# Order of the mixers turned: MLA and NSA after S5, both GDN halves last, with a new arena map

## The chip, the cores and the metric

One core of a Trainium2 chip runs the whole program. The metric is device time in microseconds (us) of one execution; lower is better. Engines by their names in the profile: PE (TensorE matmul), PEld (its weight loads), DVE (VectorE), ACT (ScalarE), POOL (GpSimd), SP (SyncE, which issues the DMAs).

## The reference, cut to what matters

Two layers, each with a token mixer and a gated convolutional MLP ("FFN") between sandwich norms. 256 tokens, width 2048, all f32. In the token mixer one projection feeds four independent groups, and one output projection takes all four:

```python
proj = h @ w_in
(cq, ckv, kpe, u_s5, nq, kc, vc, ks, vs, kw, vw, ngate, gq, gk, gv, gz, ga, gb) = split_cols(proj, IN_SIZES)
o_a = mla_mixer(cq, ckv, kpe, ...)      # latent attention: two norms, q and kv up-projections, softmax attention
o_b = s5_mixer(u_s5, ...)               # diagonal complex scan
o_c = nsa_mixer(nq, kc, vc, ks, ...)    # compressed, selected and window attention, gated
o_d = gdn_mixer(gq, gk, gv, gz, ga, gb) # conv+silu of q, k, v; chunked gated delta rule; out norm * silu(gz)
o = concat([rms_norm(o_a), rms_norm(o_b), rms_norm(o_c), o_d]) @ w_out
```

The four groups depend on `proj` alone, so any order of them computes the same.

## The kernel before, in words

**Big products.** Weights come in blocks of 512 KB (`wload`, SP's queue, 4 buffers `raw`), are split into a high and a low part (`split`: ACT casts, L423; DVE subtracts, L424; 3 buffers each) and go through PE three times (`mm3`). A *unit* here is a pair of 128-column blocks of `w_in` (`gemm_b`, L709): 16 k-steps x 2 x 3 = 96 matmuls of 256 columns into one of the four PSUM banks `mm`. A 512-column token-major product (`gemm_a`, L743) is two units. Per layer: U 2 units, GDN's q, k, v 6, its gate GZ 2, CQ 2.5, NQ 2, the shared kv columns 3.3. The output projection (`project_out`, L1548) is 32 blocks of 12 matmuls of 512 columns, in two halves `jp`; in each half the four groups come in a fixed order, and all four banks are held until the last group is done.

**Mixers** (`mixers`, L1473). S5 first, then the kv products, GDN's decay gates and NSA's compression of keys and values (`nsa_compress`, L914), then `gdn_half` (L1078) for heads 0, 1 and for heads 2, 3, then `mla` (L830), `nsa` (L962), and the GZ products with `gdn_out_gate` (L1218). In layer 0 the first two U units and three of GDN's units (`FIRST`) are computed in the opening, interleaved with the conditioning products, and their convolutions (`conv_silu`, L1025) come before S5; in layer 1 one of GDN's units is.

**What sets the order.** The program's order gives each instruction its priority; the scheduler that lays down each engine's fixed queue takes what is ready, earliest in the program first. Weight loads and splits are raised above the rest. Small PSUM work draws from `self.mx()` (L233): lane 0 and lane 1 have two banks each, and with `self.lane = None` the calls alternate, beginning with lane 1. GDN half 0 and MLA are on lane 0, GDN half 1 on lane 1; NSA starts on lane 1 and turns to None (L1005) before its window attention. From there it draws ten banks: six in `attn_probs`, two for its output, and `ss` and `R` of its norm (`norm_T`, L762). Small SBUF tiles come from pools of two buffers per name and width; the three row norms of a GDN half (`normed(1)`, `normed(0)`, the output norm; `row_rs`, L557) all take `rv`, `ry`, `ra` of width 4, those of MLA, NSA and S5 the same of width 2.

**Arena.** One SBUF tensor is mapped by hand. GDN half 0 and S5 share `A_GA`, half 1 and NSA share `A_GB`; MLA lies over `A_SIL0` and `A_GA`, so it waits for half 0, as NSA waits for half 1. Conditioning of later blocks (`ada`, DVE multiply-adds with a DMA each) is fed in by `tick` (L406), at rates per weight load, per GDN product and per attention step.

```python
        for hp in range(2):
            self.lane = hp
            self.gdn_half(l, hp, self.reg((A_GA, A_GB)[hp], 6160), qkv(hp), G, on[hp])
```

Of the kernel before, what the change touches and what calls it, by code (L numbers as in the profile page):

```python
# [12 lines left out]
F32 = mybir.dt.float32  # L13
# [3 lines left out]
AF = mybir.ActivationFunctionType  # L17
ALU = mybir.AluOpType
# [14 lines left out]
O_CQ, O_CKV, O_KPE, O_U, O_NQ, O_KC = 0, 384, 640, 704, 1216, 1728  # L33
O_NG, O_GQ, O_GK, O_GV, O_GZ, O_GA = 2496, 2508, 3020, 3532, 4044, 4556
# [16 lines left out]
A_SIL0 = A_KVT + 1704  # L51
A_GA = A_SIL0 + 1536
# [7 lines left out]
A_GP = A_SIL1  # L60
FIRST = (O_U, O_U + 256, O_GQ, O_GK, O_GV)
PAIRS = FIRST + tuple(c + 256 for c in FIRST[2:]) + (O_GZ, O_GZ + 256, O_CQ, O_CQ + 256)
TOKEN_MAJOR = (((O_KC, 426),), ((O_KC + 426, 354), (O_GA, 8), (O_KPE, 64)), ((O_NQ, 512),))
# [41 lines left out]
def blocks():  # L105

    B = {nm: Blocks() for nm in ("w_in", "w_out", "ffn_w_in", "ffn_w_out", "w_ada", "mla_w_uq", "mla_w_ukv")}
    for c0 in PAIRS:
        for k0 in range(0, KT, 4):
            B["w_in"].add(k0, 4, (c0, 256))  # L110
    for k0 in range(0, KT, 8):
        B["w_in"].add(k0, 8, (O_CQ + 512, P))
    for segs in TOKEN_MAJOR:
# [79 lines left out]
class Ker:  # L193
# [515 lines left out]
    def gemm_b(self, l, c0, nm=2):  # L709


        return self.finish(self.gemms_b(l, [(c0, self.mmt())], nm, KT))[0]

# [7 lines left out]

    def gemms_b(self, l, cols, nm, kc, tiles=False):


        kn = 1024 // (nm * P)
        parts = [[b[:, m * 256:(m + 1) * 256] for m in range(nm)] for _, b in cols]
        for kk in range(0, KT, kc):
            for (c0, _), ps in zip(cols, parts):
                for k0 in range(kk, kk + kc, kn):
                    w = self.wtile(self.blk("w_in", l, k0, kn, (c0, nm * P)))  # L730
                    for ki in range(kn):
# [182 lines left out]
    def nsa_compress(self, l, r, kvt, kT, kc, vb):  # L914


        nc, I = self.nc, self.I
        scr = r(192)
        for tt in range(2):
            v = kvt[:, tt, 0:768].rearrange("p (a b) -> p a b", a=3)[:, :, 0:32]  # L920
            self.rope(scr, v, v, self.rcos[:, tt, 32:48], self.rsin[:, tt, 32:48], 3, 16)
        kcT, vT = r(256), r(256)
        for j, o in ((KV_KC, kcT), (KV_VC, vT), (KV_KS, kT[:, 0]), (KV_KW, kT[:, 1])):
# [4 lines left out]
        for nm, src in (("k", kcT), ("v", vT)):  # L928
            w2 = r(P)
            nc.sync.dma_start(w2, I["nsa_w2_" + nm][l])  # L930
            st = r(16, 18)
# [7 lines left out]
            ab = r(256)[:18]  # L939
# [4 lines left out]
            a = r(2, 18)  # L944
# [3 lines left out]
            h, g = r(16), r(16)  # L948
            nc.vector.memset(h, 0.0)
# [268 lines left out]
    def gdn_out_gate(self, ps, out):  # L1218

        nc = self.nc  # L1220
        th = self.small.tile([P, 256], F32, name="gth", tag="gth")
        nc.scalar.activation(th, ps, AF.Tanh, scale=0.5)
        nc.vector.scalar_tensor_tensor(th, th, 1.0, ps, op0=ALU.add, op1=ALU.mult)
        nc.vector.tensor_tensor(out, out, th, op=ALU.mult)

# [241 lines left out]
    def first_gemms(self, l):  # L1467
        if l:
            return self.gemms_b(l, [(c, self.mmt()) for c in FIRST[:3]], 2, KT // 4)
        self.lane = 0  # L1470
        return self.gemms_b(l, [(c, self.mmt() if i < 4 else self.mx()) for i, c in enumerate(FIRST)], 2, KT // 4, True)

    def mixers(self, l, first):  # L1473
# [5 lines left out]
        Uc = r5(8, P)  # L1479
        u0, u1, *first_qkv = self.finish(first)  # L1480
        us = (u0, u1)
        for c2, ps in enumerate(us):
            for j in range(2):
                self.s5_gather(Uc, ps[j], 2 * c2 + j)

        def conv(hp, i, ps):
            s = self.reg((A_SIL0, A_SIL1)[hp] + i * 512, 512)(2, 256)
            for j in range(2):
                self.conv_silu(l, ps[j], 4 * i + 2 * hp + j, s[:, j])
            return s  # L1490

        early = [conv(0, i, ps) for i, ps in enumerate(first_qkv)] if l == 0 else []
        self.lane = 0
# [13 lines left out]
        self.lane = 1  # L1507
        self.nsa_compress(l, self.reg(A_OT + 1024, 3072), kvt, kT, kc, vb)

        def qkv(hp):  # L1510
            sil = list(early) if hp == 0 else []
            for i in range(len(sil), 3):
                sil.append(conv(hp, i, first_qkv[i] if i < len(first_qkv) and hp == 0 else
                                self.gemm_b(l, (O_GQ, O_GK, O_GV)[i] + hp * 256)))
            return sil


        on = [oT["gdn"][:, hp * 512:(hp + 1) * 512] for hp in range(2)]
        for hp in range(2):
            self.lane = hp  # L1520
            self.gdn_half(l, hp, self.reg((A_GA, A_GB)[hp], 6160), qkv(hp), G, on[hp])

        self.lane = 0
        cqn = [oT["mla"][:, j * 256:(j + 1) * 256] for j in range(4)]
        cqn.append(self.ar[:, A_GB + 6160:A_GB + 6416])
        for c, nm in ((0, 2), (2, 2), (4, 1)):
            ps = self.gemm_b(l, O_CQ + c * P, nm=nm)
            for j in range(nm):
                nc.scalar.copy(cqn[c + j], ps[j])
        self.mla(l, cqn, self.reg(A_SIL0, 7696), kvt, oT["mla"])  # L1530
# [239 lines left out]
```

## Time and profile before

| | us |
|---|---|
| median of 3 runs | 2710.53 (2709.11 to 2710.61) |
| the profiled execution: its time / span of its instructions | 2708.32 / 2706.5 |
| PE busy / PEld busy | 2579.7 (95%) / 2283.8 (84%) |
| DVE busy / ACT busy | 1909.8 (71%) / 1258.6 (47%) |
| mean granted TensorE clock | 0.979 of full |

The span runs: opening to about 200 us, mixers and output projection of layer 0 to 640, its FFN to about 1420, mixers and output projection of layer 1 to 1920, its FFN to the end. Busy time of PE is time covered by at least one matmul, so it is not PE at its peak. A mean over the span mixes these stages; the mixers are read stretch by stretch below.

### The profile page before, as it was taken

Reading aid. Unit: us, or ns where it says so; the run is one execution under the profiler, and the core shown is the slowest. Engines: PE = TensorE matmul, PEld = TensorE weight load, DVE = VectorE, ACT = ScalarE, POOL = GpSimd, SP = SyncE. Lnnn points to the kernel's source line nnn. Section 1 sums busy time; section 2 is a strip of 40 time slices with the busy share of each in tenths; the row PEclk is TensorE's granted clock in tenths of the full one; section 3 lists DMA queues with packets and bytes.
Section 4 is the critical chain, followed back from the end, with each engine's and each line's share of the span. In section 5 each row is a group of like instructions: output and inputs, shape, how many; then the busy total and the mean of one; then the engine's idle time right before and its main releaser. Section 6 shows DMA issues by size and latency. Waiting matters only on the chain. (4 is left out here: it accounts for less than half of the span.)

```text
span 2706.5 us, 44498 instructions
## 1 busy us (share of the span) xinstructions
PE 2579.7 (95%) x17604; PEld 2283.8 (84%) x17604; DVE 1909.8 (71%) x3018; ACT 1258.6 (47%) x2001; POOL 10.2 (0%) x22
## 2 busy tenths in 40 slices
PE   7889998888999999999998999999899999999998
PEld 3468787767999999988787879888799999998886
DVE  7348877778887777776877888865777655555555
ACT  2334354555545444444545445465544444444443
POOL 0000000000000000000000000000000000000000
PEclk9989999889999999999999999999999999999999
DMA  8676666676887888876676567735587655555554
GB/s 316 245 261 217 223 211 208 205 267 219 294 299 275 282 292 295 286 252 232 232 262 219 186 206 256 247 126 179 178 279 275 212 186 180 186 180 187 187 188 147
DMA packets 171264, 620.89 MB, mean 229 GB/s; under 512 B 19440, under 2 KB 20272, under 8 KB 169520
## 3 DMA queue, kind: packets, MB, share of 16 engines
q1 hardware_dynamic: 170048, 617.00, 66.2%
q8 instruction: 138, 2.26, 0.3%
q10 hardware_dynamic: 1008, 1.06, 0.1%
q14 instruction: 70, 0.57, 0.1%
HBM read 613.75 MB, written 4.23 MB: 228 GB/s over the span
## 5 line engine op out<-in xcount | busy, mean ns | idle before, releaser
L228 PE MATMUL mm<-ht,wh 128*128 128x256 f32 x7168 | 1316.5, 284 | 6.2 <-ACT ht L423 6.2
L423 ACT CAST wh<-raw 128x1024 fp32r<-128x1024 f32 (+1 forms) x740 | 771.7, 1044 | 964.1 <-PE mm L228 794.6
L424 DVE TENSOR_TENSOR wl<-raw,wh 128x1024 fp32r<-128x1024 f32 (+1 forms) x740 | 896.1, 1214 | 409.9 <-ACT wh L423 407.4
L228 PEld LDWEIGHTS mm<-ht,wh 128*128 128x128 f32 x7168 | 1112.8, 189 | 23.0 <-ACT ht L423 9.0
L228 PE MATMUL mm<-ht,wl 128*128 128x256 f32 x3584 | 1018.1, 284 | 0.1
L228 PEld LDWEIGHTS mm<-ht,wl 128*128 128x128 f32 x3584 | 677.5, 189 | 10.9 <-issue 6.3
L228 PE MATMUL mm<-wh,ht 128*128 128x512 f32 (+1 forms) x1600 | 504.2, 394 | 7.2 <-ACT ht L423 4.5
L462 DVE SCALAR_TENSOR_TENSOR acc<-rawa,condc,acc 128x1024 f32<-128x1024 f32 x300 | 384.5, 1282 | 148.1 <-DMA rawa<-in_w_ada_dram 146.7
L228 PEld LDWEIGHTS mm<-wh,ht 128*128 128x128 f32 x1600 | 300.7, 189 | 71.5 <-ACT ht L423 4.8
L228 PE MATMUL mm<-wl,ht 128*128 128x512 f32 (+1 forms) x800 | 314.9, 394 | 1.0 <-DVE wl L424 1.0
L228 PE MATMUL mx<-wh,ht 128*128 128x512 f32 x704 | 222.3, 396 | 0.0
L228 PE MATMUL mx<-arena 128*128 128x128 f32 (+8 forms) x1432 | 200.8, 284 | 9.9 <-ACT arena L1464 2.9
L228 PEld LDWEIGHTS mx<-arena 128*128 128x128 f32 (+5 forms) x1432 | 158.7, 173 | 51.0 <-issue 15.4
L228 PEld LDWEIGHTS mm<-wl,ht 128*128 128x128 f32 x800 | 151.4, 189 | 33.5 <-DVE wl L424 2.2
L228 PEld LDWEIGHTS mx<-wh,ht 128*128 128x128 f32 x704 | 132.6, 188 | 32.3
L228 PE MATMUL mx<-wl,ht 128*128 128x512 f32 x352 | 139.7, 397 | 0.8 <-DVE wl L424 0.8
L424 DVE TENSOR_TENSOR ht<-arena,ht 128x1024 fp32r<-128x1024 f32 x52 | 63.6, 1223 | 39.9 <-ACT ht L423 39.6
L1607 DVE SCALAR_TENSOR_TENSOR arena<-mm,vec,arena 128x255 f32<-128x255 f32 (+1 forms) x176 | 78.3, 476 | 6.2 <-ACT arena L1605 5.3
L228 PEld LDWEIGHTS mx<-wl,ht 128*128 128x128 f32 x352 | 66.3, 188 | 17.3 <-DVE wl L424 1.2
L423 ACT CAST ht<-arena 128x1024 fp32r<-128x1024 f32 x52 | 54.1, 1049 | 56.7 <-PE mm L228 31.4
L228 PE MATMUL mx<-rawm,arena 128*18 128x256 f32 (+3 forms) x248 | 74.5, 494 | 2.1 <-DMA rawm<-in_w_ada_dram 1.3
L232 PE MATMUL mx<-ident,arena 128*128 128x128 f32 (+1 forms) x328 | 59.7, 286 | 11.5 <-ACT arena L807 5.6
(315 smaller groups left out, 1550.6 us busy)
## 6 DMA issues: line engine op xcount, KB each, us to landing
raw<-in_ffn_w_in_dram SPq DMA_DIRECT2D x352, 512.0 KB, 4.3
rawa<-in_w_ada_dram SPq DMA_DIRECT2D x344, 512.0 KB, 5.0
raw<-in_ffn_w_out_dram SPq DMA_DIRECT2D x176, 512.0 KB, 4.3
raw<-in_w_in_dram SPq DMA_DIRECT2D x116, 512.0 KB, 4.3
raw<-in_w_out_dram SPq DMA_DIRECT2D x64, 512.0 KB, 4.2
raw<-in_w_in_dram SPq DMA_DIRECT2D x32, 426.0 KB, 4.1
rawm<-in_w_ada_dram SPq DMA_DIRECT2D x20, 512.0 KB, 6.0
acc<-in_w_ada_dram SPq DMA_DIRECT2D x20, 512.0 KB, 6.9
```

The lines of the kernel that those rows point to most:

```text
L228: self.nc.tensor.matmul(out, lhsT=lhsT, rhs=rhs, start=start, stop=stop)
L232: self.nc.tensor.transpose(out, in_, self.ident[:k, :k])
L423: self.nc.scalar.copy(hi.bitcast(F32R), src)
L424: self.nc.vector.tensor_sub(lo.bitcast(F32R), src, hi)
L462: self.nc.vector.scalar_tensor_tensor(acc, w, self.condc[:, kc:kc + 1], acc, op0=ALU.mult, op1=ALU.add)
L1607: nc.vector.scalar_tensor_tensor(c[:, s:], ps[m][:, :256 - s], self.fconv(l, 2 - s, f), c[:, s:], op0=ALU.mult, op1=ALU.add)
```

## The change

After it the order is: U and CQ in the opening (layer 0 all of CQ, layer 1 its first unit), S5, kv products, compression, the rest of CQ, NQ, `mla` (lane 0), `nsa` (lane 1), then the six GDN units with their convolutions, both `gdn_half` (lane 0, lane 1), GZ, and one multiply per half by the gate. MLA and NSA get regions of their own (`A_MLA`, `A_NSA`), and the GDN halves take those regions over. Compression works in `A_SIL0` with one set of scratch for keys and values, and its small matrix comes through `rawm` in place of a direct load. The 128-column block of CQ is loaded in four pieces in place of two. The output projection takes NSA before GDN. `mla`, `nsa` and `gdn_half` themselves are not touched.

```diff
-FIRST = (O_U, O_U + 256, O_GQ, O_GK, O_GV)
+FIRST = ((O_U, 2), (O_U + 256, 2), (O_CQ, 2), (O_CQ + 256, 2), (O_CQ + 512, 1))
+A_MLA, A_NSA, A_SILB = A_GA, A_GA + 6656, A_GA + 12544
+A_GATE = (A_GA + 5888, A_SILB + 1536)
...
-    for k0 in range(0, KT, 8):
-        B["w_in"].add(k0, 8, (O_CQ + 512, P))
+    for k0 in range(0, KT, 4):
+        B["w_in"].add(k0, 4, (O_CQ + 512, P))
...
     def nsa_compress(self, l, r, kvt, kT, kc, vb):
-        scr = r(192)
+        STN = 18
+        kcT, vT, st_, ab_, rest = r(256), r(256), r(16 * STN), r(256), r(72)
+        scr = st_
...
-            w2 = r(P)
-            nc.sync.dma_start(w2, I["nsa_w2_" + nm][l])
...
+            w2 = self.mload(I["nsa_w2_" + nm][l])
...
     def gdn_out_gate(self, ps, out):
         nc = self.nc
-        th = self.small.tile([P, 256], F32, name="gth", tag="gth")
-        nc.scalar.activation(th, ps, AF.Tanh, scale=0.5)
-        nc.vector.scalar_tensor_tensor(th, th, 1.0, ps, op0=ALU.add, op1=ALU.mult)
-        nc.vector.tensor_tensor(out, out, th, op=ALU.mult)
+        nc.scalar.activation(out, ps, AF.Tanh, scale=0.5)
+        nc.vector.scalar_tensor_tensor(out, out, 1.0, ps, op0=ALU.add, op1=ALU.mult)
...
     def first_gemms(self, l):
         if l:
-            return self.gemms_b(l, [(c, self.mmt()) for c in FIRST[:3]], 2, KT // 4)
+            return self.gemms_b(l, [c + (self.mmt(),) for c in FIRST[:3]], KT // 4)
...
     def mixers(self, l, first):
-        u0, u1, *first_qkv = self.finish(first)
+        cqn = [oT["mla"][:, j * 256:(j + 1) * 256] for j in range(4)] + [oT["gdn"][:, 0:256]]
+        u0, u1, *done = self.finish(first)
...
-        early = [conv(0, i, ps) for i, ps in enumerate(first_qkv)] if l == 0 else []
+        for i, ps in enumerate(done):
+            latents(i, ps)
         self.lane = 0
         self.s5(l, r5, Uc, oT["s5"])
...
-        self.nsa_compress(l, self.reg(A_OT + 1024, 3072), kvt, kT, kc, vb)
-        for hp in range(2):
-            self.lane = hp
-            self.gdn_half(l, hp, self.reg((A_GA, A_GB)[hp], 6160), qkv(hp), G, on[hp])
-        self.lane = 0
-        for c, nm in ((0, 2), (2, 2), (4, 1)):
-            ps = self.gemm_b(l, O_CQ + c * P, nm=nm)
-            for j in range(nm):
-                nc.scalar.copy(cqn[c + j], ps[j])
-        self.mla(l, cqn, self.reg(A_SIL0, 7696), kvt, oT["mla"])
-        self.lane = 1
+        self.nsa_compress(l, self.reg(A_SIL0, 1536), kvt, kT, kc, vb)
+        for i in range(len(done), 3):
+            latents(i, self.gemm_b(l, *FIRST[2 + i]))
         nq = oT["nsa"].rearrange("p (a b) -> p a b", a=2)
         ps = self.gemm_a(l, TOKEN_MAJOR[2])
         for tt in range(2):
             nc.scalar.copy(nq[:, tt], ps[tt])
-        self.nsa(l, self.reg(A_GB, 6160), nq, kvt, kT, kc, vb, oT["nsa"])
+        self.lane = 0
+        self.mla(l, cqn, self.reg(A_MLA, 6656), kvt, oT["mla"])
+        self.lane = 1
+        self.nsa(l, self.reg(A_NSA, 5888), nq, kvt, kT, kc, vb, oT["nsa"])
+
+        sil = []
+        for hp in range(2):
+            r = self.reg((A_SIL0, A_SILB)[hp], 1536)
+            sil.append([])
+            for i, c0 in enumerate((O_GQ, O_GK, O_GV)):
+                ps = self.gemm_b(l, c0 + hp * 256)
+                t = r(2, 256)
+                for j in range(2):
+                    self.conv_silu(l, ps[j], 4 * i + 2 * hp + j, t[:, j])
+                sil[hp].append(t)
+        on = [oT["gdn"][:, hp * 512:(hp + 1) * 512] for hp in range(2)]
+        for hp in range(2):
+            self.lane = hp
+            self.gdn_half(l, hp, self.reg((A_MLA, A_NSA)[hp], 5888), sil[hp], G, on[hp])
         self.lane = None
+        gate = []
         for hp in range(2):
+            gate.append(self.reg(A_GATE[hp], 512)(512))
             ps = self.gemm_b(l, O_GZ + hp * 256)
             for j in range(2):
-                h = 2 * hp + j
-                og = oT["gdn"][:, h * 256:(h + 1) * 256]
-                self.gdn_out_gate(ps[j], og)
+                self.gdn_out_gate(ps[j], gate[hp][:, j * 256:(j + 1) * 256])
+        for hp in range(2):
+            nc.vector.tensor_tensor(on[hp], on[hp], gate[hp], op=ALU.mult)
...
     def project_out(self, l, oT):
-        order = (("s5", 4), ("mla", 0), ("gdn", 12), ("nsa", 8))
+        order = (("s5", 4), ("mla", 0), ("nsa", 8), ("gdn", 12))
```

## Rows read from the trace of the kernel before

**Rows 1.** Windows, layers 0 and 1: us, then busy PE, PEld, DVE, ACT, POOL, clock, DMA.

```profile
425.00:505.00 80.00, 70.35 (x468) 58.22 (x467) 60.27 (x157) 37.16 (x94) 0.96 (x1) 0.94 0.59 202
...
505.00:586.00 81.00, 62.53 (x379) 51.51 (x378) 63.42 (x160) 45.13 (x108) 2.27 (x2) 0.85 0.72 246
...
1605.00:1716.00 111.00, 110.03 (x892) 100.86 (x891) 93.52 (x168) 63.13 (x133) 0.53 (x1) 1.00 0.78 262
...
1716.00:1786.00 70.00, 69.06 (x498) 59.23 (x498) 54.76 (x144) 32.32 (x72) 0.00 (x0) 1.00 0.63 212
...
1786.00:1853.00 67.00, 66.83 (x458) 58.13 (x458) 37.66 (x103) 45.64 (x112) 0.00 (x0) 1.00 0.37 129
```

**Rows 2.** Timeline, layer 0, norms of the GDN halves: start us, us, engine, line.

```profile
359.54 0.27 ACT L652 ACTIVATE junk<-mx 128x128 bf16<-128x128 f32 x1
...
410.46 0.16 DVE L559 TENSOR_SCALAR rv<-mx 128x4 f32<-128x4 f32 x1 [2.45 <-PE mx L228]
...
410.54 0.16 DVE L559 TENSOR_SCALAR rv<-gss 128x4 f32<-128x4 f32 x1
```

**Rows 3.** Timeline, layer 1, DVE: the same two norms.

```profile
1702.84 0.16 DVE L559 TENSOR_SCALAR rv<-mx 128x4 f32<-128x4 f32 x1
...
1702.91 0.16 DVE L559 TENSOR_SCALAR rv<-gss 128x4 f32<-128x4 f32 x1
```

**Rows 4.** Timeline, layer 0, PE and ACT at the front of NSA.

```profile
504.68 1.06 PE L228 MATMUL mx<-nkc,arena 128*128 128x16 f32 x8 [0.19 <-DVE arena L1216]
...
505.54 0.57 ACT L978 COPY arena<-mx 128x512 f32<-128x512 f32 x1
...
519.91 0.31 PE L232 MATMUL mx<-ident,arena 128*128 128x128 f32 x1
...
520.06 0.96 PE L228 MATMUL mx<-nkc,arena 128*128 128x16 f32 x8
...
525.25 0.64 PE L228 MATMUL mx<-arena 128*128 128x128 f32 x2
```

**Rows 5.** Timeline, layer 0, DVE: where row norms begin (rv) and end (ry).

```profile
330.58 0.16 DVE L256 SCALAR_TENSOR_TENSOR ry<-ra,ry 128x2 f32<-128x2 f32 x1
...
423.50 0.15 DVE L256 SCALAR_TENSOR_TENSOR ry<-ra,ry 128x4 f32<-128x4 f32 x1
...
427.40 0.16 DVE L559 TENSOR_SCALAR rv<-mx 128x2 f32<-128x2 f32 x1 [1.61 <-PE mx L228]
...
500.88 0.15 DVE L256 SCALAR_TENSOR_TENSOR ry<-ra,ry 128x4 f32<-128x4 f32 x1
...
525.27 0.16 DVE L256 SCALAR_TENSOR_TENSOR ry<-ra,ry 128x2 f32<-128x2 f32 x1
...
581.62 0.16 DVE L256 SCALAR_TENSOR_TENSOR ry<-ra,ry 128x2 f32<-128x2 f32 x1
```

**Rows 6.** Timeline, layer 1, DVE: the same row norms.

```profile
1602.68 0.16 DVE L256 SCALAR_TENSOR_TENSOR ry<-ra,ry 128x2 f32<-128x2 f32 x1
...
1713.18 0.16 DVE L256 SCALAR_TENSOR_TENSOR ry<-ra,ry 128x4 f32<-128x4 f32 x1
...
1719.30 0.16 DVE L559 TENSOR_SCALAR rv<-mx 128x2 f32<-128x2 f32 x1 [1.57 <-PE mx L228]
...
1784.29 0.16 DVE L256 SCALAR_TENSOR_TENSOR ry<-ra,ry 128x4 f32<-128x4 f32 x1
...
1817.95 0.16 DVE L256 SCALAR_TENSOR_TENSOR ry<-ra,ry 128x2 f32<-128x2 f32 x1
...
1852.50 0.16 DVE L256 SCALAR_TENSOR_TENSOR ry<-ra,ry 128x2 f32<-128x2 f32 x1
```

**Rows 7.** Chain that ended last, layer 1, output projection: start us, us, what.

```profile
1853.49 35.37 PE mm L228 x151
```

**Rows 8.** Line 1032, convolutions of GDN: duration ns min/median/max.

```profile
L1032 DVE SCALAR_TENSOR_TENSOR arena<-mx,vec,arena x6: 471/476/478, 198.8 to 211.4; 128x255 f32<-128x255 f32 x2, 128x254 f32<-128x254 f32 x2, 128x253 f32<-128x253 f32 x2
```

**Rows 9.** DMA issues: KB each, median us to landing.

```profile
arena<-in_nsa_w_k_dram SPq DMA_DIRECT2D x2, 64.0 KB, 3.9
```

More of the change, by code (lines that the diff above doesn't have):

```diff
@@ L60 @@
 A_GP = A_SIL1
-FIRST = (O_U, O_U + 256, O_GQ, O_GK, O_GV)
-PAIRS = FIRST + tuple(c + 256 for c in FIRST[2:]) + (O_GZ, O_GZ + 256, O_CQ, O_CQ + 256)
+FIRST = ((O_U, 2), (O_U + 256, 2), (O_CQ, 2), (O_CQ + 256, 2), (O_CQ + 512, 1))
+PAIRS = (O_U, O_U + 256, O_CQ, O_CQ + 256) + tuple(c + d for c in (O_GQ, O_GK, O_GV, O_GZ) for d in (0, 256))
+A_MLA, A_NSA, A_SILB = A_GA, A_GA + 6656, A_GA + 12544
+A_GATE = (A_GA + 5888, A_SILB + 1536)
 TOKEN_MAJOR = (((O_KC, 426),), ((O_KC + 426, 354), (O_GA, 8), (O_KPE, 64)), ((O_NQ, 512),))
@@ L709, in gemm_b @@
     def gemm_b(self, l, c0, nm=2):
-        return self.finish(self.gemms_b(l, [(c0, self.mmt())], nm, KT))[0]
+        return self.finish(self.gemms_b(l, [(c0, nm, self.mmt())], KT))[0]
     @staticmethod
@@ L720, in finish, with gemms_b @@
                 return e.value
-    def gemms_b(self, l, cols, nm, kc, tiles=False):
-        kn = 1024 // (nm * P)
-        parts = [[b[:, m * 256:(m + 1) * 256] for m in range(nm)] for _, b in cols]
+    def gemms_b(self, l, cols, kc, tiles=False):
+        parts = [[b[:, m * 256:(m + 1) * 256] for m in range(nm)] for _, nm, b in cols]
         for kk in range(0, KT, kc):
[L728 to L731, printed above, removed]
+            for (c0, nm, _), ps in zip(cols, parts):
+                for k0 in range(kk, kk + kc, 4):
+                    w = self.wtile(self.blk("w_in", l, k0, 4, (c0, nm * P)))
+                    for ki in range(4):
                         k = k0 + ki
@@ L928, in nsa_compress @@
         for nm, src in (("k", kcT), ("v", vT)):
-            w2 = r(P)
-            nc.sync.dma_start(w2, I["nsa_w2_" + nm][l])
-            st = r(16, 18)
+            st = st_.rearrange("p (q n) -> p q n", n=STN)
             nc.vector.tensor_copy(st[:, :, 0:16], src.rearrange("p (m q) -> p q m", q=16))
@@ L938, in nsa_compress @@
                     self.mm(acc[:18], st[:, q0 + q], raw[:, q * 256:(q + 1) * 256], q0 + q == 0, q0 + q == 15)
-            ab = r(256)[:18]
+            w2 = self.mload(I["nsa_w2_" + nm][l])
+            ab = ab_[:18]
             nc.scalar.copy(ab, acc[:18])
@@ L943, in nsa_compress @@
                 self.tp(psT[:, i * 32:i * 32 + 18], ab[:, i * P:(i + 1) * P])
-            a = r(2, 18)
+            a = rest[:, 0:36].rearrange("p (i n) -> p i n", i=2)
             nc.vector.tensor_copy(a, psT[:, 0:64].rearrange("p (i n) -> p i n", i=2)[:, :, 0:18])
@@ L947, in nsa_compress @@
             nc.vector.tensor_tensor(pc, a[:, 0, 16:17], a[:, 1, 17:18], op=ALU.add)
-            h, g = r(16), r(16)
+            h, g = rest[:, 36:52], rest[:, 52:68]
             nc.vector.memset(h, 0.0)
@@ L1468, in first_gemms @@
         if l:
-            return self.gemms_b(l, [(c, self.mmt()) for c in FIRST[:3]], 2, KT // 4)
+            return self.gemms_b(l, [c + (self.mmt(),) for c in FIRST[:3]], KT // 4)
         self.lane = 0
-        return self.gemms_b(l, [(c, self.mmt() if i < 4 else self.mx()) for i, c in enumerate(FIRST)], 2, KT // 4, True)
+        return self.gemms_b(l, [c + (self.mmt() if i < 4 else self.mx(),) for i, c in enumerate(FIRST)], KT // 4, True)
     def mixers(self, l, first):
@@ L1479, in mixers, with latents @@
         Uc = r5(8, P)
-        u0, u1, *first_qkv = self.finish(first)
-        us = (u0, u1)
-        for c2, ps in enumerate(us):
+        cqn = [oT["mla"][:, j * 256:(j + 1) * 256] for j in range(4)] + [oT["gdn"][:, 0:256]]
+        u0, u1, *done = self.finish(first)
+        for c2, ps in enumerate((u0, u1)):
             for j in range(2):
                 self.s5_gather(Uc, ps[j], 2 * c2 + j)
[L1486 to L1490, printed above, removed]
-        early = [conv(0, i, ps) for i, ps in enumerate(first_qkv)] if l == 0 else []
+        def latents(i, ps):
+            for j, p in enumerate(ps):
+                nc.scalar.copy(cqn[2 * i + j], p)
+        for i, ps in enumerate(done):
+            latents(i, ps)
         self.lane = 0
@@ L1507, in mixers @@
         self.lane = 1
-        self.nsa_compress(l, self.reg(A_OT + 1024, 3072), kvt, kT, kc, vb)
[L1510 to L1518, printed above, removed]
-        for hp in range(2):
-            self.lane = hp
-            self.gdn_half(l, hp, self.reg((A_GA, A_GB)[hp], 6160), qkv(hp), G, on[hp])
-        self.lane = 0
-        cqn = [oT["mla"][:, j * 256:(j + 1) * 256] for j in range(4)]
-        cqn.append(self.ar[:, A_GB + 6160:A_GB + 6416])
-        for c, nm in ((0, 2), (2, 2), (4, 1)):
-            ps = self.gemm_b(l, O_CQ + c * P, nm=nm)
-            for j in range(nm):
-                nc.scalar.copy(cqn[c + j], ps[j])
-        self.mla(l, cqn, self.reg(A_SIL0, 7696), kvt, oT["mla"])
-        self.lane = 1
+        self.nsa_compress(l, self.reg(A_SIL0, 1536), kvt, kT, kc, vb)
+        for i in range(len(done), 3):
+            latents(i, self.gemm_b(l, *FIRST[2 + i]))
         nq = oT["nsa"].rearrange("p (a b) -> p a b", a=2)
```

1 line of the change is left out of this document (removed).

## The prediction, made before the changed kernel was run

> **What bounds the kernel now.** The windows of PE over the mixers come first, because the change moves work only there. In layer 1 PE is busy 110.0 of 111, 69.1 of 70 and 66.8 of 67 us [rows 1]: product work fills nearly every wait, and an order of the mixers can give back some 2 us. In layer 0 it is busy 70.4 of 80 and 62.5 of 81 us, 28.1 us idle, at a clock of 0.94 and 0.85: here a chain of dependent small steps decides.
>
> Next I read that chain by its row norms, each of which ends a mixer. Layer 0 [rows 5]: S5 330.58, GDN half 0 423.50, half 1 500.88, MLA 525.27, NSA 581.62. Layer 1 [rows 6]: 1602.68, 1713.18, 1784.29, 1817.95, 1852.50. So from S5 to NSA the stages are 92.9 + 77.4 + 80.7 = 251.0 us and 110.5 + 71.1 + 68.2 = 249.8 us. The two halves stand one behind the other, though they have different banks, regions and inputs.
>
> The third view, the timeline around that seam, says why. In layer 0 the squares of half 1's first norm are done at 359.8, but the norm's first step on DVE starts at 410.54, 0.08 us after the first step of half 0's *output* norm at 410.46 [rows 2]. In layer 1 the same pair is 0.07 us apart, at 1702.84 and 1702.91 [rows 3]. Both draw `rv` of width 4 from a pool of two. Half 0's first `rv` was long free; half 1's (the fourth of that name) is still not handed out before the third. I read this as: buffers of one name are handed out strictly in program order. The PSUM lanes show it too. At the front of NSA the second token tile's scores (520.06) start right behind the transpose of the first tile (519.91), though their query was copied at 505.54 and one bank of the lane was free; the first selected attention follows at 525.25 [rows 4].
>
> **The change part by part.**
>
> *The halves at the end.* `gdn_half` and its names are unchanged, so half 1 still starts its first norm at half 0's output norm. "Side by side" remains one after the other. Half 1 costs 77.4 or 71.1 us from norm to norm; I take 72, the stretch with less in its way, for it will run last, against few competitors.
>
> *Half 0 behind NSA.* Half 0 draws from lane 0. NSA, before it in the program, turns to alternating lanes for its second attention: six banks, two for its output, `ss` and `R`; beginning with lane 1, the tenth, `R`, is on lane 0 in layer 0. By the rule just read, half 0's first transposes wait for `R`, so for NSA's last norm, though its region is free when MLA ends. In layer 1 the count may put `R` on lane 1, and half 0 starts at `ss`, somewhat sooner; I put nothing for that. From its start half 0 takes between 71.1 (half 1 in layer 1) and 110.5 (half 0 there, under the full load of products); I take 78, nearer the light end, since GDN's units are done by then and GZ and the output projection are left.
>
> *MLA beside NSA.* MLA took 97.9 and 98.7 us from the start of its first norm to the end of its last [rows 5, 6], with half 1 ahead of it in priority. Now it is first: above 99, below 79 (a fifth off, about the spread of half 0 between the layers, 92.9 to 110.5, taken as what load does to such a chain). I take 85. NSA's scores and selected attention run beside it on lane 1, but the window attention needs lane 0 behind MLA's last bank. From MLA's last norm to NSA's took 34.6 us in layer 1 and 56.4 in layer 0, where the selected attention came late; I take 35.
>
> *Sum of the chain.* 85 + 35 + 78 + 72 = 270 us from S5's norm to half 1's, against 251.0 and 249.8: **+19** and **+20** us. All lower ends give 79 + 35 + 71 + 71 = 256 (+5, +6), all upper ends 99 + 56 + 110 + 77 = 342 (+91, +92).
>
> *What hides in it.* A matmul of 512 columns takes 35.37/151 = 0.234 us in the output projection [rows 7], so one of 256 some 0.117, a unit 11.2 and a group of a projection half (48 matmuls) 11.2. Six GDN units (67 us) can run early, four of them in the free banks during S5. What can run under the halves is GZ (22 us) and three groups of the projection's first half (34 us). In layer 1 that no longer fills two stretches of 70 to 80 us: PE should idle there for tens of us, where it idled 2.
>
> *The convolutions.* In layer 0 six of them leave the place ahead of S5: 6 x 4 operations of 0.476 us [rows 8] = 11.4 us of DVE. S5's chain lives on DVE, so it can end up to 11 us sooner; lower bound nothing, I take 8. The opening also loses half a unit (5.6 us of PE) to a later stage; the opening has idle PE, the later stage is held by its chain, so it is put at nothing, and at 5.6 if PE binds there.
>
> *Small edits.* Two more, smaller loads of CQ per layer move the same bytes. The small compression matrix goes through `rawm` behind four large loads instead of directly: it holds one of two buffers for a while, and the second set of weights then comes through one buffer; a load lands in 3.9 us [rows 9], so some 4 x 3.9 = 16 us later at worst, all under S5's chain; without that cover NSA's front would be 16 us late. Shared scratch for keys and values puts the second behind the first under the same cover. On SP's queue the reload of `x` and the gate row now wait for the halves instead of MLA and NSA; weight loads are raised ahead of them, as before. The gate product shrinks to one multiply per half beside the same split that followed NSA's norm: nothing.
>
> *Sum.* +19 - 8 + 20 = +31 us on the profiled execution's 2708.3, 2739 us; it stood 2.2 us below the median, so I predict 2741.
>
> A rule speaks about how much PE has to give. The PEld column covers 109.7 of the 161 us of layer 0 and 218.2 of the 248 us of layer 1 [rows 1], less than PE does. The Trainium skill, Perfetto Trace Analysis, "Identifying the Most-Contended Engine", says that matmul busy time is no measure of the distance to the limit and weight-load busy time is; no run here yet shows which of the two is right for these stretches.
>
> **The rivals.**
>
> 1. *The halves do overlap* (another order of allocation would do). For it: regions, banks and inputs are separate. Against it: the pairs 0.08 and 0.07 us apart [rows 2, 3]. The pair would cost one loaded half: 85 + 35 + 110 = 230, so -21 - 8 in layer 0 and at most -2 in layer 1: 2680 on the median. Chance 0.08.
> 2. *Fill decides, not the chain*: GDN's units fill MLA's and NSA's waits, and layer 0's 28.1 idle us are recovered; 2682. It ends on the faster side. It decides if PE stays busy under the last half, which needs products left over for it. For it: layer 1 is filled today. Against it: the work is spent earlier. Chance 0.10.
> 3. *The ends cancel*: the low end of the chain, 256 us: +5 - 8 + 6 = +3, 2714, which is no change. Chance 0.14.
> 4. *Hidden slack*: PE waits inside its busy time, and denser filling under MLA and NSA recovers it. At most 51.3 + 29.8 = 81 us [rows 1], 2629; against it, a block of 512-column matmuls runs back to back at 0.234 us [rows 7]. It is the case that the skill's rule above would make. Chance 0.04.
>
> **How the numbers follow.** Forecast, slower: 0.64, own range 2716 to 2790 (the upper ends of both layers are not reached together; I take somewhat under half of +183). A measurement of this kernel can tell about 0.2%, 5.4 us, from no change. Faster 0.08 + 0.10 + 0.04 = 0.22, same 0.14, slower 0.64. The range 2681 to 2790 takes in rivals 2 and 3; rivals 1 and 4 and some 0.06 above it are left out.
>
> **What would show it.** Right: half 1's first `rv` again starts within 0.1 us of half 0's output norm in both layers; half 0's first norm begins only after NSA's last in layer 0; PE busy falls well under 90% during half 1 in layer 1, at a lower clock; the MLA stretch is under 97.9 us. Wrong: norms of the two halves that interleave (rival 1), or PE above 95% in the last stretch (rival 2). If S5 in layer 0 ends no sooner than before against the opening, the 8 us fall; if MLA's stretch is longer than 99 us, the priority argument does.

## The result: 79 us slower, a ratio of 1.028

The kernel after took 2789.5 us (median of four runs, 2784.0 to 2792.7), beside 2710.6 for the kernel before on the same chip: a ratio of 1.0282, 95% interval 1.0259 to 1.0306. The forecast was 2741 us, range 2681 to 2790: the sign and its cause held, the size was 79 us in place of +31. In the profiled executions the span grew from 2706.5 to 2785.7 us, by 79.2.

First the windows of the kernel after, one for each stage of the chain, which answer to [rows 1] (us, then busy PE, PEld, DVE, ACT, POOL, clock, DMA share, GB/s). Layer 0 goes from S5's norm at 301 to half 1's at 604, layer 1 from 1652 to 1936.

```profile
301.00:396.00 95.00, 93.47 (x672) 82.31 (x670) 76.05 (x191) 50.38 (x119) 0.95 (x1) 0.99 0.68 225
396.00:430.00 34.00, 34.00 (x297) 33.32 (x296) 31.66 (x67) 18.82 (x41) 0.00 (x0) 1.00 0.73 242
430.00:460.00 30.00, 28.76 (x222) 27.37 (x222) 28.46 (x49) 17.47 (x31) 0.00 (x0) 1.00 0.88 306
460.00:478.00 18.00, 18.00 (x83) 14.01 (x82) 17.03 (x27) 10.65 (x30) 0.00 (x0) 1.00 0.90 312
478.00:530.00 52.00, 41.96 (x277) 34.69 (x276) 17.95 (x46) 20.59 (x43) 0.00 (x0) 0.86 0.39 126
530.00:604.00 74.00, 46.09 (x254) 38.48 (x255) 36.88 (x64) 24.18 (x67) 2.33 (x2) 0.59 0.38 123
1652.00:1745.00 93.00, 92.36 (x667) 82.82 (x666) 77.23 (x199) 53.32 (x117) 0.00 (x0) 1.00 0.75 246
1745.00:1781.00 36.00, 35.41 (x307) 34.37 (x307) 27.16 (x59) 19.67 (x45) 0.00 (x0) 1.00 0.49 160
1781.00:1876.00 95.00, 89.16 (x630) 77.29 (x629) 65.70 (x119) 50.93 (x104) 0.00 (x0) 0.99 0.65 218
1876.00:1936.00 60.00, 37.52 (x254) 31.74 (x254) 16.49 (x51) 18.62 (x51) 0.00 (x0) 0.78 0.03 9
```

PE is full up to the middle of half 0, and VectorE nearly so (28.46 of 30 us, 17.03 of 18). Then the supply of product work ends, and half 1 runs alone. In layer 0 all of it runs under half 0: from 430 to 530 us PE does 192 matmuls of 256 columns, the two units of GZ, and 144 of 512, the three groups of the output projection (the rows are the products with the weights' high part; those with the low part are half as many); from 530 to 604 there is none of either.

```profile
L230 PE MATMUL mm<-wh,ht 128*128 128x512 f32 x96 | 32.0, 406 | 1.1 <-DVE ht L426 1.1
L230 PE MATMUL mm<-ht,wh 128*128 128x256 f32 x128 | 23.8, 284 | 0.0
```

Under half 1 PE is busy 46.1 of 74 and 37.5 of 60 us at a clock of 0.59 and 0.78. The transfers have stopped too (9 GB/s in layer 1).

The timeline of the kernel after has the row norms that end the stages (S5, MLA, NSA, half 0, half 1), as in [rows 5, 6], the first step of MLA's first norm (`rv` of width 2), and the two pairs of [rows 2, 3]. First layer 0, VectorE.

```profile
301.37 0.16 DVE L258 SCALAR_TENSOR_TENSOR ry<-ra,ry 128x2 f32<-128x2 f32 x1
...
311.24 0.16 DVE L561 TENSOR_SCALAR rv<-mx 128x2 f32<-128x2 f32 x1
...
396.27 0.15 DVE L258 SCALAR_TENSOR_TENSOR ry<-ra,ry 128x2 f32<-128x2 f32 x1
...
429.63 0.16 DVE L258 SCALAR_TENSOR_TENSOR ry<-ra,ry 128x2 f32<-128x2 f32 x1
...
527.70 0.16 DVE L561 TENSOR_SCALAR rv<-mx 128x4 f32<-128x4 f32 x1 [5.37 <-PE mx L230]
527.78 0.16 DVE L561 TENSOR_SCALAR rv<-gss 128x4 f32<-128x4 f32 x1
...
529.92 0.28 DVE L258 SCALAR_TENSOR_TENSOR ry<-ra,ry 128x4 f32<-128x4 f32 x2
...
603.70 0.16 DVE L258 SCALAR_TENSOR_TENSOR ry<-ra,ry 128x4 f32<-128x4 f32 x1
```

Then layer 1, the same engine.

```profile
1652.36 0.16 DVE L258 SCALAR_TENSOR_TENSOR ry<-ra,ry 128x2 f32<-128x2 f32 x1
...
1666.99 0.15 DVE L561 TENSOR_SCALAR rv<-mx 128x2 f32<-128x2 f32 x1
...
1744.93 0.16 DVE L258 SCALAR_TENSOR_TENSOR ry<-ra,ry 128x2 f32<-128x2 f32 x1
...
1780.59 0.16 DVE L258 SCALAR_TENSOR_TENSOR ry<-ra,ry 128x2 f32<-128x2 f32 x1
...
1874.26 0.16 DVE L561 TENSOR_SCALAR rv<-mx 128x4 f32<-128x4 f32 x1 [3.74 <-PE mx L230]
1874.34 0.16 DVE L561 TENSOR_SCALAR rv<-gss 128x4 f32<-128x4 f32 x1
...
1876.48 0.28 DVE L258 SCALAR_TENSOR_TENSOR ry<-ra,ry 128x4 f32<-128x4 f32 x2
...
1936.38 0.16 DVE L258 SCALAR_TENSOR_TENSOR ry<-ra,ry 128x4 f32<-128x4 f32 x1
```

Half 1's first norm starts 0.08 us behind the start of half 0's output norm in both layers. The stages, as differences of these rows, beside the forecast's terms:

| us | forecast | layer 0 | layer 1 |
|---|---|---|---|
| MLA behind S5 | 85 | 94.9 | 92.6 |
| NSA behind MLA | 35 | 33.4 | 35.7 |
| half 0 behind NSA | 78 | 100.3 | 95.9 |
| half 1 behind half 0 | 72 | 73.8 | 59.9 |
| sum | 270 | 302.3 | 284.0 |
| against before | +19, +20 | +51.3 | +34.2 |

The rest of the 79.2 us (the feed-forward block is taken from its first matmul): S5's norm in layer 0 ends 29.2 us sooner (301.4 against 330.6); from the chain's end to the feed-forward block of layer 0 it takes 81.1 us in place of 73.1 (+8.0), that block +2.0; from there to S5's norm in layer 1 178.9 in place of 161.3 (+17.6); behind the chain of layer 1 -4.6.

### The profile page after: what moved, and what is told of

It reads as the page before. It is cut to its first block, busy times and chain, and to the rows that moved or that the text cites. A ratio compares the mean times of both kernels' runs of the same rounds, so it can differ in the third digit from the quotient of the medians.

```text
span 2785.7 us, 44541 instructions
## 1 busy us (share of the span) xinstructions
PE 2613.4 (94%) x17604; PEld 2309.1 (83%) x17604; DVE 1912.2 (69%) x3018; ACT 1258.6 (45%) x2006; POOL 10.7 (0%) x22
## 4 chain that ended last, share of the span: by engine, by line
PE 81%; DVE 7%; DMA 6%; ACT 3%; issue 2%; SPq 0%; DVEq 0%; ACTq 0%
PE mm L230 58%; PE mx L230 21%; DMA rawa<-in_w_ada_dram 5%; DVE wl L426 2%; PE mx L234 2%; ACT wh L425 1%; DVE acc L464 1%; DVE arena L1358 1%; DVE arena L1090 1%; ACT junk L654 0%; DMA rawm<-in_mla_w_uq_dram 0%; DVE arena L1238 0%; DMA vec<-in_vec_dram 0%; ACT arena L1121 0%; DMA rawm<-in_nsa_w_v_dram 0%
## 5 line engine op out<-in xcount | busy, mean ns | idle before, releaser
L230 PE MATMUL mm<-wh,ht 128*128 128x512 f32 (+1 forms) x1600 | 512.9, 398 | 6.7 <-ACT ht L425 4.7
L230 PE MATMUL mx<-arena 128*128 128x128 f32 (+7 forms) x1424 | 216.3, 301 | 25.2 <-ACT arena L1121 8.7
L230 PEld LDWEIGHTS mx<-arena 128*128 128x128 f32 (+4 forms) x1424 | 171.6, 188 | 70.2 <-issue 18.8
L234 PEld LDWEIGHTS mx<-ident,arena 128*128 128x128 f32 (+1 forms) x328 | 41.3, 152 | 48.0 <-ACT arena L1100 12.2
L230 PE MATMUL mx<-rawm,arena 128*18 128x256 f32 (+4 forms) x252 | 75.7, 500 | 4.7 <-DMA rawm<-in_w_ada_dram 2.0
```

Source lines behind the costliest of these rows:

```text
L230: self.nc.tensor.matmul(out, lhsT=lhsT, rhs=rhs, start=start, stop=stop)
L234: self.nc.tensor.transpose(out, in_, self.ident[:k, :k])
```

## Experiments

**1. Small tiles named apart by half** (kernel after).

```diff
-            ss = self.sm(4, "gss%d" % i)
+            ss = self.sm(4, "gss%d_%d" % (i, hp))
-            r = self.row_rs(ss, 1.0, 4e-6)
+            r = self.row_rs(ss, 1.0, 4e-6, "h%d" % hp)    # rv, ry, ra + "h0" or "h1"
...
-        r = self.row_rs(b4(ss)[:, :, 0], P)
+        r = self.row_rs(b4(ss)[:, :, 0], P, h="h%d" % hp)
```

> The kernel after the change, with names of their own for the small norm tiles of each GDN half (rv, ry, ra and the sums gss). Theory 1 (buffers of one name are handed out in program order, and the chain of mixers sets the end): half 1's first norm starts within some 20 us of its squares, long before half 0's output norm, and the two output norms come within 30 us of each other; of the 73.8 and 59.9 us that half 1 adds behind half 0, 30 to 45 us per layer go, so the run takes 2700 to 2730 us. Rival (half 1 waits for DVE or PE time, or for data): its first norm stays within a microsecond of half 0's output norm, time within 5 us of 2789.

Measured: 2704.8 us, 0.997 of before (0.9959 to 0.9982), 85 us under the kernel after. Its timeline on VectorE, layer 0: the last of the halves' four input norms, then the ends of the two output norms.

```profile
484.35 0.16 DVE L561 TENSOR_SCALAR rvh<-gss 128x4 f32<-128x4 f32 x1
...
529.94 0.17 DVE L258 SCALAR_TENSOR_TENSOR ryh<-rah,ryh 128x4 f32<-128x4 f32 x1
...
553.37 0.16 DVE L258 SCALAR_TENSOR_TENSOR ryh<-rah,ryh 128x4 f32<-128x4 f32 x1
```

All four input norms are under way 45 us ahead of the end of half 0's output norm, and half 1 ends 23 us behind half 0 in place of 73.8 (25 in place of 59.9 in layer 1). The shared names kept the halves in series. Half 0 itself is no faster: 106 us behind NSA's norm.

**2. Only the reciprocal square root's names apart** (rv, ry, ra; the sums of squares shared again).

> Of the names that were set apart by half in the run of 2704.8 us, only those of the reciprocal square root (rv, ry, ra) are; the sums of squares of both halves share their tiles again. Theory: the two tiles of rv are what ties half 1 to half 0's last norm, so the outputs of the halves lie 20-35 us apart as they did there (23 and 25), total 2697-2713 us. Rival: the shared sums tie as well; then 55-75 us apart, total 2765-2795.

Measured: 2704.0 us, 0.9957 of before (0.9941 to 0.9973); the outputs 26 us apart in both layers. The tie is `rv` and its two companions; the three were not told apart.

**3. The same names in the kernel before.**

> The kernel before the change with the same names of their own. Theory 1: in layer 0 half 1's first norm starts near 360 us instead of 410.5, NSA starts 20 to 50 us earlier, and layer 0 gains 10 to 40 us; layer 1 has PE full and gains 3 us at most: 2670 to 2700 us. Rival: no change, 2706 to 2715 us.

Measured: 2698.9 us, 0.9944 of before (0.9923 to 0.9965). Its timeline, layer 0, VectorE: ends of the output norms of half 0, half 1 and NSA.

```profile
415.97 0.15 DVE L256 SCALAR_TENSOR_TENSOR ryh<-rah,ryh 128x4 f32<-128x4 f32 x1
...
453.87 0.16 DVE L256 SCALAR_TENSOR_TENSOR ryh<-rah,ryh 128x4 f32<-128x4 f32 x1
...
556.48 0.16 DVE L256 SCALAR_TENSOR_TENSOR ry<-ra,ry 128x2 f32<-128x2 f32 x1
```

Half 1 comes 47 us and NSA 25 us sooner than in [rows 5], and the kernel gains 0.6%; layer 0's feed-forward block, up to layer 1's first matmul, takes 801.9 us in place of 786.7. The same edit is worth 3% in the order after, where no products are left to run beside a lone half; that this makes the difference is a reading, not a run.

**4. NSA on one lane** (kernel after; `self.lane = None` inside NSA dropped). It was to tell whether NSA's last bank holds half 0.

> The kernel after the change, with NSA kept on lane 1 to its end, so that lane 0 is free once MLA has drawn its last bank. Theory 1: in layer 0 half 0's first transposes start near MLA's end (396 us) instead of behind NSA's last norm (430 us); the window attention, with one lane, gets slower by 5 to 15 us; net 10 to 25 us less per layer, 2740 to 2770 us. Rival (half 0 is held by its convolutions and by products on PE, not by the lane): half 0's output norm stays within 5 us of 530 and the time within 10 us of 2789 or above.

Measured: 2804.4 us, 1.0343 of before (1.0324 to 1.0363), 15 us over the kernel after. Half 0's first transposes come at 429.8 us, 0.9 us ahead of NSA's last spread (431.2 and 1.3 us behind it in the kernel after), its first norm at 434.2 (437.4). So the lane is not what held half 0. The profiled execution was 23.8 us longer than that of the kernel after: layer 0's feed-forward block +6.1, in layer 1 the stretch up to NSA's norm +5.2 and half 1 +8.4. What makes them stays open.

**5. GDN's six units written ahead of MLA** (kernel after).

> The kernel after the change, with the six GDN units and their convolutions written ahead of MLA, so that they have priority over MLA and NSA. If half 0's 100.3 and 95.9 us (78 forecast) are long because units and convolutions still run under it, the stretch from NSA's last norm to half 0's falls to 75 to 85 us, MLA's stretch grows by 5 to 20 us, and the time falls by 10 to 40 us. If they are long because of the output projection's splits and the conditioning steps under it, the stretch stays within 5 us of 100 and 96 and the time rises.

Measured: 2879.8 us, 1.0616 of before (1.0593 to 1.0638). Half 0 ends 71.5 us behind NSA in layer 0 (100.3 after), as expected. But MLA's first norm starts only at 375.8 us (311.2 after) and takes its last step at 381.7, for the units fill PE first. The window from S5's norm to there, and that of half 0 later:

```profile
300.00:381.00 81.00, 81.00 (x674) 78.35 (x673) 73.46 (x114) 39.48 (x62) 0.00 (x0) 1.00 0.83 285
...
499.00:570.00 71.00, 49.41 (x286) 40.81 (x286) 24.88 (x73) 26.20 (x72) 0.00 (x0) 0.79 0.30 99
```

Product work that is done early is missing later: in layer 0 PE idles here in every stage from MLA on, 49.4 of 71 us busy in half 0. GZ had run earlier too, its last product read at 456.4 us, so that half 0's 71.5 us (65.8 in layer 1) are those of a half with little to run beside it. What stands earlier in the program goes first on a full PE.

**6. Conditioning out of half 0.** In the kernel after, groups of VectorE's instructions from 430 to 478 us, the input norms of half 0 in layer 0 (out<-in, count | busy us, mean ns | idle before):

```profile
L426 DVE TENSOR_TENSOR wl<-raw,wh 128x1024 fp32r<-128x1024 f32 x15 | 18.2, 1222 | 0.3 <-ACT wh L425 0.2
L464 DVE SCALAR_TENSOR_TENSOR acc<-rawa,condc,acc 128x1024 f32<-128x1024 f32 x12 | 15.4, 1283 | 1.9 <-DMA rawa<-in_w_ada_dram 1.9
```

The first norm starts at 437.35 and its last step comes at 459.60: 22 us for thirteen steps of 0.16 us, queued behind weight splits and conditioning multiply-adds of 1.2 to 1.3 us. The edit takes the latter away:

```diff
+        self.bg_rate = 0.0                       # for the six GDN units
...
-            self.tick(self.rates[1])
+            self.tick((0.0, 2 * self.rates[1] + 1.2 * self.rates[0])[hp])
```

> The kernel after, with the background conditioning blocks taken out of the six GDN units and out of half 0 and put into half 1 (about 24 of its 1.28 us multiply-adds in layer 0, 16 in layer 1). Theory A, a crowded VectorE: from 430 to 478 us of layer 0 VectorE was 95% busy, with 15 weight splits of 1.22 us and 12 multiply-adds of 1.28 us in front of the 0.16 us operations of half 0's first two norms, so half 0's stretch behind NSA falls from 100.3 to 80-88 us in layer 0 and from 95.9 to 82-90 in layer 1; half 1's stretch, 73.8 and 59.9 us, grows by 0-6. Total 2750-2785 us. Rival, the order of TensorE's queue: TensorE was full (28.8 of 30 us) with the fill itself, and half 0's matmuls stand behind it, so VectorE's share falls but the stretches stay within 4 us of 100.3 and 95.9; total 2780-2800.

Measured: 2778.7 us, 1.025 of before (1.0231 to 1.0268). Its windows for half 0 and half 1, layer 0, then half 0 of layer 1:

```profile
417.00:498.00 81.00, 80.45 (x615) 72.08 (x616) 49.66 (x112) 47.23 (x102) 0.00 (x0) 1.00 0.44 151
498.00:567.00 69.00, 50.18 (x327) 41.58 (x327) 37.44 (x65) 28.35 (x73) 2.33 (x2) 0.75 0.43 142
...
1780.00:1865.00 85.00, 84.30 (x647) 75.97 (x647) 50.89 (x114) 49.06 (x103) 0.00 (x0) 1.00 0.47 151
```

The first norm now takes 6.7 us (431.45 to 438.11), half 0's stretch 81.0 in layer 0 (100.3) and 84.8 in layer 1 (95.9): theory A. Half 1 did not pay for it in layer 0 (69.4 us, 73.8 after) and little in layer 1 (62.5, 59.9). The stretch from MLA's norm to NSA's fell as well, to 22.2 and 26.2 us (33.4 and 35.7), for the units whose conditioning was taken away run there; so the load was not half 0's alone. Layer 0's chain ends 36.8 us sooner, yet the total keeps 11: PE waits 63.0 us at the feed-forward block, in two pieces of 24.9 and 38.1, for conditioning values (DVE, line 485).

**7. The same with the names apart.**

> The same move of the conditioning, in the kernel after with the small tiles named apart by half (2704.8 us by itself). Theory A: the two norms of half 0 took 424 to 476 us in layer 0 there, with VectorE 95% busy; they shorten by 10-20 us, and the last chain ends sooner by as much in layer 0 and by 5-10 us in layer 1: 2670-2695 us. Rival, order on TensorE: 2698-2715 us, and the pair of half outputs stays at about 106 and 129 us after NSA's norm in layer 0.

Measured: 2712.8 us, 0.9996 of before (0.9983 to 1.0009), no better than the names alone. Layer 0's last chain ends at 530.9 us (553.4 with the names), and then this is PE's largest wait between 613 and 677 us (us in total, times, longest):

```profile
PE mx L230 <- DVE acc L485: 57.4, 2, 37.7
```

The mechanism of theory A holds and its gain is gone: in layer 0 the conditioning is itself due at the feed-forward block. The total follows the rival, for another reason than the one it gave.

**8. Names apart, conditioning late in layer 1 alone.**

> The kernel after with the small tiles named apart by half (2704.8 us), and with the conditioning put into half 1 in layer 1 alone. In layer 0 the same move had the feed-forward block wait 57.4 us for conditioning values; in layer 1 it had brought the chain from S5's norm to the last half's output from 249.1 to 233.1 us and given back 5.4 before the feed-forward block. Theory: that is a crowded VectorE in the norms of half 0, so layer 1 keeps some 10 us: 2688-2698 us. Rival: the gain is only put off here too, since the conditioning has to run somewhere ahead of the feed-forward block: 2700-2712 us.

Measured: 2689.0 us, 0.9896 of before (0.9878 to 0.9913), the fastest here, ahead of both kernels. Its timeline, layer 1: end of S5's norm and of half 1's.

```profile
1614.20 0.16 DVE L258 SCALAR_TENSOR_TENSOR ry<-ra,ry 128x2 f32<-128x2 f32 x1
...
1847.30 0.16 DVE L258 SCALAR_TENSOR_TENSOR ryh<-rah,ryh 128x4 f32<-128x4 f32 x1
```

That chain is 233.1 us long (249.1 with the names alone), and from the first matmul of the layer to that of its feed-forward block 488.2 (497.8). This 10 us is what the trace shows; the ratios differ by some 20, and the profiled execution (2703.4) was among its slower ones.

**9. Six convolutions put back ahead of S5** (kernel after, layer 0, results thrown away).

> The kernel after with six convolutions of 128x256 added in layer 0 ahead of S5, on the products that S5 and MLA use, their results thrown away: what the kernel before had there. Theory: each costs VectorE 3 x 0.48 + 0.42 us, 11 us together, between the opening and S5's first scans, so S5's norm ends at 310-324 us in place of 301, and the total is 8-20 us above the kernel after's (2797-2810). Rival: S5's norm ended 29 us sooner for the narrower last product of the opening (its first operation came 20 us sooner, the opening's transfers 7) and VectorE has the room; then S5's norm moves by under 4 us, the total by under 5.

Measured: 2818.9 us, 1.0383 of before (1.035 to 1.0417), about 1% or 27 us over the kernel after. S5's norm ends at 325.3, so 24 of its 29 us. Groups on VectorE from 180 to 325 us:

```profile
L426 DVE TENSOR_TENSOR wl<-raw,wh 128x1024 fp32r<-128x1024 f32 (+1 forms) x34 | 38.6, 1138 | 8.5 <-ACT wh L425 8.4
...
L1033 DVE SCALAR_TENSOR_TENSOR arena<-mm,vec,arena 128x255 f32<-128x255 f32 (+2 forms) x24 | 10.5, 470 | 0.1
L1036 DVE SCALAR_TENSOR_TENSOR arena<-gth,arena 128x256 f32<-128x256 f32 x8 | 3.2, 419 | 1.0 <-ACT gth L1035 1.0
```

Of these eight convolutions six are the added ones, from 181 to 205 us, some 10 us of VectorE; the other two are GDN's own, from 307 us on. VectorE waits 8.4 us for ScalarE's part of the weight splits (1.8 in the kernel after from 180 to 301): they cost on both engines, and the run does not part the two. The size is above what was expected.

**10. The early convolutions of the kernel before written behind S5.**

> The kernel before, with layer 0's early convolutions of the first half written behind S5 instead of ahead of it; nothing else. Theory: the S5 norm of layer 0 ends 29.2 us sooner in the kernel after (301.4 against 330.6) because no convolution stands ahead of S5 on ScalarE and VectorE; so here S5's norm ends at 305-318 us, and of that the layer keeps half or less, since half 0 now starts with its convolutions: total 2692-2710 us. Rival: the earlier S5 comes from the narrower last product of the opening and the work on TensorE that is no longer there; then S5's norm moves by less than 6 us (325-331), total within 4 us of the kernel before.

Measured: 2713.4 us, 1.0009 of before (0.9993 to 1.0024), S5's norm at 335.1. The edit didn't move the work: VectorE's steps of all six still ran between 191 and 224 us (189 to 214 before), since they were ready and S5's steps left room. It decides nothing; experiment 9 is what bears on it.

**11. The compression's clearing moved to GpSimd** (kernel after), for the 17.6 us ahead of S5's norm in layer 1.

> The kernel after, with the clearing of the compression's 16-column scratch moved from VectorE to GpSimd. Theory: in layer 1 that clearing waits for the old residual in the same arena columns, and VectorE's queue with S5's work waits behind it; so layer 1's opening with S5, 178.9 us in the kernel after and 161.3 before, falls by 3-7 us, layer 0 stays, and the total falls by 2-6 us (2782-2788). Rival: VectorE waits there for other work of the same region, and the opening stays within 1.5 us of 178.9, the total within 2 us of the kernel after.

Measured: 2790.5 us, 1.0293 of before (1.0271 to 1.0315); the opening with S5 is 178.2 us: the rival. What the 17.6 us are, the groups of PE show, from the layer's first matmul to S5's norm. The kernel after has two forms there that the kernel before has not:

```profile
L230 PE MATMUL mm<-wh,ht 128*128 128x512 f32 x48 | 16.5, 410 | 0.0
...
L230 PE MATMUL mm<-wl,ht 128*128 128x512 f32 x24 | 10.0, 417 | 0.0
```

These 72 matmuls of 512 columns, 26.5 us, stand against 36 fewer of 256 columns: three quarters of NSA's query product, which the change writes ahead of MLA, ran here. PE's busy time in the stretch rose from 156.5 to 173.7 us. It is work brought forward, not a stall.

**12. Half 0 ahead of half 1's units** (the kernel of experiment 8). In the kernel after the timeline of layer 0 has NSA's last spread, half 0's first transposes and the evacuation of the sixth GDN unit side by side:

```profile
429.89 0.66 PE L230 MATMUL mx<-ident,ry 128*128 128x128 f32 x4
...
431.16 0.66 PE L234 MATMUL mx<-ident,arena 128*128 128x128 f32 x4
...
431.32 0.45 ACT L1031 ACTIVATE arena<-mm,vec 128x256 f32<-128x256 f32 x1
```

> The run with names apart and the conditioning of layer 1 in half 1 (2689.0 us), with half 0 written behind its own three GDN units and ahead of those of half 1. Where half 0 starts: in the kernel after its first transposes come at 431.16 us, 0.2 us ahead of the evacuation of the sixth unit (431.32) and 1.3 us behind NSA's last spread (429.89); with the conditioning moved away they came at 428.46, again 1 us ahead of the sixth unit's evacuation and 11.6 us behind NSA's spread. Theory: the six units stand ahead of half 0 on TensorE, which is full, and not NSA's last bank; then half 0's first norm now starts ahead of NSA's last norm in both layers, 10-30 us sooner than there (433.3 and 1753.0 us), and its output norm 10-25 us sooner; the total gains less, as half 1 comes behind its own units: 2675-2695 us. Rival: NSA's last norm or its lane holds half 0 (as the prediction had it); then half 0's first norm stays behind NSA's last norm in layer 0, and the total within 5 us of 2689.

Measured: 2715.7 us, 1.0005 of before (0.9991 to 1.0018), 1% slower than experiment 8. First steps of NSA's last norm and of half 0's first, layer 0, then layer 1:

```profile
412.24 0.16 DVE L561 TENSOR_SCALAR rv<-mx 128x2 f32<-128x2 f32 x1 [0.27 <-PE mx L230]
...
419.15 0.16 DVE L561 TENSOR_SCALAR rvh<-gss 128x4 f32<-128x4 f32 x1
...
1739.55 0.16 DVE L561 TENSOR_SCALAR rv<-mx 128x2 f32<-128x2 f32 x1 [2.46 <-PE mx L230]
1740.43 0.17 DVE L561 TENSOR_SCALAR rvh<-gss 128x4 f32<-128x4 f32 x1
```

Half 0's first norm comes 14 and 13 us sooner than in experiment 8. In layer 1 it overlaps NSA's norm (ended at 1741.8), where it stood 18.7 us behind: there the units of half 1 had held it. The rows of layer 0 of experiment 6 read the same way: NSA's norm ended at 416.6, and half 0's first transposes came only at 428.5, 1 us ahead of the sixth unit's evacuation. With these units written later, layer 0 has half 0's first norm 3.7 us behind NSA's (ended at 415.4), 7.2 in experiment 8: a second gate, for which the rival fits; in the kernel after the two gates lay 1.4 us apart. The halves' outputs in layer 0 now lie 83 us apart (492.4 and 575.4; 26 in experiment 8), with half 1 alone at a clock of 0.59 from 540 to 580 us: the time is back where the change had it.

## Why the prediction was right in sign and short in size

**Right.** *The halves stay one behind the other*: 0.08 us in both layers, and experiments 1 and 2 show that the cause is the named one, the names that the halves share. (That buffers go out strictly in program order is the reading that fits; no run tests it by itself.) Undoing it takes the whole loss away: with the names apart the kernel after is 85 us faster. NSA behind MLA (35) and half 1 behind half 0 in layer 0 (72) were measured at 33.4 to 35.7 and 73.8. PE fell to 37.5 of 60 us in the last stretch of layer 1 at a lower clock, as listed. Half 0's first norm began only after NSA's last, as listed too, but that was luck: the bank and lane named for it were not what held it (experiment 4).

**The step that failed: "half 0 behind NSA", taken at 78 us, "nearer the light end, since GDN's units are done by then".** Half 0 took 100.3 and 95.9 us, the loaded end of the range that the prediction itself gave (110.5). The units' products were indeed nearly done, at about 430 us in layer 0, but what was left was not light. The prediction had counted GZ and three groups of the projection, 56 us, as filler under both halves; in layer 0 all of it ran under half 0 and none under half 1, with PE busy 46.8 and VectorE 45.5 of the 48 us from 430 to 478. Where the filler had been spent before, half 0 took 71.5 us (experiment 5). Two things are shown to make up the length. The input norms' small steps queue on VectorE behind splits and conditioning; taking the latter away shortened the stretch by 19.3 and 11.1 us (experiment 6). And half 0 starts behind the last units on a full PE, its first norm 7.7 and 11.2 us behind NSA's (experiments 6 and 12); the prediction named NSA's last bank, which may hold it next in layer 0, but not by the lane (experiment 4). "Against few competitors" was true of half 1, not of half 0. This step is 40 of the missing 48 us.

**MLA, taken at 85: a term left out.** The 97.9 and 98.7 us from which the 85 was taken run from the start of MLA's first norm, but the sum sets 85 behind the end of S5's. Counted from its first norm MLA took 85.0 and 77.9 us, so the size held. The 9.9 and 14.6 us between S5's norm and that start (301.37 to 311.24, 1652.36 to 1666.99) had been put at nothing without a reason: the small steps of GDN's decay gates and of NSA's compression run there, and PE is busy in all of it (9.8 of 9.8 and 14.6 of 14.6 us). In the kernel before, the like stretch was part of half 0's stage: 10.9 and 12.5 us from S5's norm to half 0's first.

```profile
341.47 0.17 DVE L559 TENSOR_SCALAR rv<-gss 128x4 f32<-128x4 f32 x1
...
1615.13 0.16 DVE L559 TENSOR_SCALAR rv<-gss 128x4 f32<-128x4 f32 x1
```

**The convolutions, -8**: -29.2, of which experiment 9 gives back 24. Only VectorE's steps of the convolutions, 11.4 us, were priced, and ScalarE's share of the same work was left out; the other 5 us stay open.

**Put at nothing:** the end of layer 0, +8.0 (from the projection's last matmul to the block's first it takes 16.6 us in place of 9.8, and three conditioning steps of 1.2 to 1.3 us stand on VectorE among those of the row norm there; not tried by itself), and the opening of layer 1, +17.6, NSA's query product brought forward. Half 1 in layer 1 gave 12 back (59.9 for 72). By the terms: forecast +31, chain +46.5 more (half 0 +40, the stretch ahead of MLA +24.5, MLA itself -7, NSA -1, half 1 -10), S5 -21, the rest +23, so +79.

**Rivals.** *The halves overlap* (0.08) priced what experiment 1 then measured, 2705 for its 2680. *Fill decides* failed on its own condition, products left over for the last half. *Hidden slack* would have shown as less busy time on PE for the same work. From layer 1's first matmul to its feed-forward block PE was busy 472.0 us before, 488.5 after, and 470.7 and 475.0 in experiments 3 and 1: no slack of 81 us came out. The rule of the Trainium skill (Perfetto Trace Analysis, "Identifying the Most-Contended Engine"), that weight-load busy time and not matmul busy time tells the distance to the limit, got no support from these runs, and none tested it by itself.

## What to carry to other kernels

Two chains meant to run side by side need buffers of their own down to the smallest name: three tiles of 4 columns cost 85 us here, and the first sight of it is one chain's first step 0.08 us behind the first step of the other chain's last norm. Independent products that a kernel uses as filler run as soon as program order lets them, so before moving a chain of small steps to the end count what will be left to run beside it, and give a chain in a filled stretch the duration of a loaded one. A duration taken from one pair of rows must stand between the same pair in the sum. Background work that is moved out of a chain's way still has its due time: in layer 0 it came back as a wait of 57 us (experiment 7), in layer 1 it paid.

## What had not been expected of the hardware

Small VectorE steps in a row cost as much as what is queued between them. Half 0's first norm in layer 0, thirteen steps of 0.16 us, took 22.4 us in the kernel after and 6.8 in experiment 6; VectorE was busy 21.55 and 6.64 us of it, so full both times, with 38 instructions in the one stretch and 22 in the other. A busy share would not have told the two apart.

The lone half was longer in the main where the granted clock was lower. Half 1 took 73.8, 69.4, 62.5 and 59.9 us where its stretch had a granted clock of 0.59, 0.75, 0.85 and 0.78 (experiment 6 for the middle two), means between the levels of 1.2 and 2.4 GHz; PE had been busy 42.0 of the 52 us before the first of them, 89.2 of 95 before the last. The order is not strict, what runs beside half 1 differs too, and no run changed the clock alone; so how much is the clock's is not shown.
